# Gating the second half's convolution branch beside the recurrence, dealing rows to 120 blocks, and norming dense tiles one by one

## The chip, the cores and the metric

One NeuronCore (core 0) of one Trainium2 chip. The metric is the device time of one launch in microseconds (us); the time before is the median of three runs.

## The reference, cut to what matters

A decoder block on 1024 tokens of width 1024 (16 meta tokens are put in front and dropped again): two token mixers side by side, a gated sum, and an expert layer.

```python
z = rmsnorm(h, g_mix) @ w_in                       # conv_val, conv_gate, rwkv_in, gate_logits
y_a = conformer_conv(conv_val, conv_gate, ...)     # ... silu(layernorm(conv(u))) @ w_conv_out
y_b = rwkv7_mix(rwkv_in, ...)                      # a recurrence over tokens, then ... @ w_rwkv_out
gate_a, gate_b = split(sigmoid(gate_logits), 2)
h = h + (gate_a * y_a + gate_b * y_b) @ w_o
h = h + peer_ffn(rmsnorm(h, g_ffn), ...)           # 8 heads x top 16 of 128x128 experts per token
out = rmsnorm(h, g_final)[:, 16:]

# peer_ffn, per token t with its 128 chosen experts e:
coef = gate * gelu(x . expert_u[e])
y = sum over e of coef * expert_v[e]
```

## The kernel before, in words

All arithmetic is fp32. A matrix product runs as three TensorE matmuls on a split of each operand into a high and a low part (`mm3`, L226 to L229). The split (`split`, L222 to L224) is a copy on ScalarE (ACT) for the high part and a subtraction on GpSimd (POOL) for the low one. `whalf` (L231) loads half of a 128-column weight tile through SyncE's DMA queue, splits it, and notes the split in a list `paces` that later paces row gathers.

The engines work through their queues in order. A scheduler writes these queues at build time: it takes instructions by the order of the program text, as priority, and by its own estimate of when they can run. Work marked `LATER` has a lower priority and fills gaps.

The tokens are taken in two halves of 512. The first half runs through convolution, recurrence, mix and routing before the second half's recurrence starts. For the second half the order in the text is: `rwkv_inputs(1)`, the recurrence `rwkv(1)` (chunks of small matmuls, L385 to L785, which ends in the tile `carry`, L744), the gates, then

- `gather_coefs` (L1015 to L1033), marked `LATER`: for token tile 3 each of 128 chosen rows of expert_u is gathered (L1027, one gather of 128 x 1024 fp32 on POOL's queue) and multiplied with x and summed on VectorE (DVE, L1029, "dot"). The first 62 rows use a pool of their own, `ga`; the other 66 use the pool `gp`.
- `mix_and_route(1)` (L849 to L975): both branches are projected. The convolution branch `sil` is loaded from DRAM and split as `s2`, the recurrence branch `ogd` as `o2`. Eight output columns m times two branches k, each 12 matmuls of 128x512, are multiplied on DVE with the gates `sga` from DRAM (L902). The k = 0 products of all eight m come first and are kept in `hbuf1`; the k = 1 products follow and are added (L912), split as `m2`, and multiplied with `w_o` (L913 to L932; the residual sum is L929). The queries and the top 16 follow.
- `gather_rows` for token tile 0 (L980 to L1013), `LATER`: per row one gather of 1 MB (expert_u and expert_v row of each of 128 tokens, L1005), a dot (L1008), gelu and gate on ACT (L1009, L1010), and the weighted sum onto `yr` (L1000, "row add"). There are three row buffers.
- `spread_gates` (L1046): gates and coefs of the other five token tiles become dense 128-expert blocks. `u_stage` for 68 blocks.
- `dense` (L1106 to L1179): 32 groups of 4 expert blocks. Per group the gated activations `c` times expert_v (`py`, `zp`, 128x512) are added onto the residual of five token tiles DT = 4, 5, 6, 7, 3 (L1161). Meanwhile the 256 rows of tiles 1 and 2 run through `gather_rows`: 8 are dealt at block 3 and 2 at every later block, so the last ones at block 127.
- The end: the rows left over, then one norm over the five dense tiles at once (L1169, `rstd` L194 to L206: Ln and Exp on ACT, then two small DVE operations), and per tile the product with `g_final`: on DVE (L1177) for t = 0, 2, 4, on ACT and POOL (L1174, L1175) for t = 1, 3. Tile 2's own norm and output (`final`, L1035 to L1043) come with its last row.

Matmuls read the sums of the two tiles `zps` and `acc`, PSUM buffers that are taken in turn.

```python
        early = range(8 * hf)
        kept = [hb1[0][:, m // 2, 512 * (m % 2):512 * (m % 2) + 512] for m in early]
        for m in early:
            mixed(m, 0, s2, kept[m])
        for m in range(8):
            ga = kept[m] if m in early else mixed(m, 0, s2, None)
            gb = mixed(m, 1, o2, None)
            V.tensor_add(gb, gb, ga)
            split(m2[:, 0, m], m2[:, 1, m], gb)
```

## Time and profile before

| what | value |
|---|---|
| time, median of three runs | 3659.9 us (3624.96 to 3678.22) |
| the profiled execution's own time | 3653.25 us |
| its span, first to last instruction | 3651.5 us |
| mean granted TensorE clock | 0.944 |
| busy: TensorE (PE), DVE, POOL, ACT | 90%, 74%, 62%, 43% |
| TensorE instructions | 16175 |

In rows of the profile a line number is one of the kernel before. PE is TensorE, DVE VectorE, ACT ScalarE, POOL GpSimd, SP SyncE. Names stand as result<-operands. In brackets is how long the engine sat idle before the instruction and what ended that. PEclk is the granted TensorE clock, 1.00 for 2.4 GHz and 0.50 for 1.2 GHz. PE's instructions overlap each other, so their starts, not their durations, give the rate.

### The profile page before, as it was taken

How to read it: one execution, taken by the hardware profiler on the slowest of the kernel's cores; microseconds unless marked ns; L12 is line 12 of the kernel's file. 1: busy time of each engine (PE TensorE's matmuls, PEld its weight loads, DVE VectorE, ACT ScalarE, POOL GpSimd, SP SyncE). 2: the span in 40 equal slices, each digit the busy share in tenths (PEclk: the TensorE clock that was granted, in tenths of full speed). 3: DMA queues.
4: the chain of work that ended last, by engine and by line, in shares of the span. 5: the costliest groups of instructions: out<-in, count | busy, mean ns of one | idle time of the engine just before them, and what ended most of it. 6: DMA issues, size and time to landing. Idle time of an engine off the chain costs nothing.

```text
span 3651.5 us, 49244 instructions
## 1 busy us (share of the span) xinstructions
PE 3282.5 (90%) x16175; PEld 2635.6 (72%) x16175; DVE 2684.8 (74%) x5108; ACT 1563.9 (43%) x3714; POOL 2280.4 (62%) x2123
## 2 busy tenths in 40 slices
PE   7999998888788998788899996899999998989994
PEld 7887776677566776676688885777777776777773
DVE  2566538969986775899999887666767666667777
ACT  5555443243444444433367774333333343333333
POOL 3442304535787655656888886676777766767774
PEclk9999979999998899999899998999999999999997
DMA  4321213333677676854699999888889888888987
GB/s 152 113 66 48 60 44 121 107 131 97 199 222 243 180 230 226 308 183 153 215 333 345 351 344 317 285 316 311 319 331 333 332 304 309 319 305 316 329 329 277
DMA packets 347381, 867.66 MB, mean 238 GB/s; under 512 B 53208, under 2 KB 132704, under 8 KB 293876
## 3 DMA queue, kind: packets, MB, share of 16 engines
q0 software_dynamic: 75328, 475.06, 36.0%
q1 hardware_dynamic: 182436, 328.77, 26.9%
q10 hardware_dynamic: 89360, 60.68, 5.4%
q8 instruction: 128, 2.10, 0.2%
q14 instruction: 129, 1.06, 0.1%
HBM read 777.48 MB, written 86.92 MB: 237 GB/s over the span
## 4 chain that ended last, share of the span: by engine, by line
PE 30%; DVE 20%; DMA 13%; issue 10%; POOL 8%; ACT 2%; POOLq 0%; ACTq 0%; DVEq 0%; SPq 0%
DMA row<-euv,idx 6%; PE zp L227 5%; PE zp L229 5%; PE zp L228 5%; PE py L227 3%; PE pg L1088 3%; PE py L228 3%; PE py L229 3%; POOL vlo L224 2%; DVE row L1008 2%; DMA gd<-gt 2%; DVE yr L1000 2%; DVE cy L348 2%; DMA vraw<-euv 2%; POOL row L1027 2%
## 5 line engine op out<-in xcount | busy, mean ns | idle before, releaser
L1005 POOL DMA_INDIRECT row<-euv,idx x384 | 411.2, 1071 | 319.6 <-DVE yr L1000 231.9
L1000 DVE SCALAR_TENSOR_TENSOR yr<-row,act,yr 128x1024 f32<-128x1024 f32 x384 | 493.2, 1284 | 153.9 <-ACT act L1010 151.6
L1008 DVE SCALAR_TENSOR_TENSOR row<-row,xr 128x1024 f32<-128x1024 f32 x256 | 311.5, 1217 | 164.4 <-DMA row<-euv,idx 157.5
L224 POOL TENSOR_TENSOR vlo<-vraw,vhi 128x512 fp32r<-128x512 f32 x256 | 330.8, 1303 | 156.7 <-ACT vhi L223 139.9
L224 POOL TENSOR_TENSOR ul<-ur,uh 128x512 fp32r<-128x512 f32 x256 | 340.3, 1336 | 38.6 <-ACT uh L223 32.2
L1009 ACT ACTIVATE act<-act 128x1 f32<-128x1 f32 x384 | 76.7, 200 | 644.2 <-DVE row L1008 635.3
L227 PE MATMUL py<-vhi,c 128*128 128x512 f32 x640 | 259.0, 409 | 75.8 <-DVE hbuf L1161 32.6
L227 PE MATMUL zp<-x,uh 128*128 128x512 f32 x784 | 315.5, 402 | 7.9 <-ACT g L1101 7.9
L229 PE MATMUL zp<-x,ul 128*128 128x512 f32 x784 | 314.4, 401 | 6.3 <-POOL ul L224 6.3
L228 PE MATMUL zp<-x,uh 128*128 128x512 f32 x784 | 314.4, 401 | 0.0
L229 PE MATMUL py<-vhi,c 128*128 128x512 f32 x640 | 255.6, 406 | 17.0 <-POOL c L224 16.7
L227 PE MATMUL zp<-vhi,c 128*128 128x512 f32 x640 | 251.4, 401 | 21.4 <-DVE hbuf L1161 15.2
L223 ACT ACTIVATE vhi<-vraw 128x512 fp32r<-128x512 f32 x256 | 159.9, 626 | 255.7 <-DMA vraw<-euv 129.4
L228 PE MATMUL py<-vlo,c 128*128 128x512 f32 x640 | 257.1, 402 | 0.4 <-POOL vlo L224 0.4
L228 PE MATMUL zp<-vlo,c 128*128 128x512 f32 x640 | 251.8, 398 | 0.0
L229 PE MATMUL zp<-vhi,c 128*128 128x512 f32 x640 | 249.3, 398 | 0.0
L348 DVE SCALAR_TENSOR_TENSOR cy<-u,vec,cy 128x512 f32<-128x512 f32 x240 | 243.4, 1014 | 5.4
L1008 DVE SCALAR_TENSOR_TENSOR row<-row,xng 128x1024 f32<-128x1024 f32 x128 | 217.4, 1700 | 14.3 <-DMA row<-euv,idx 14.3
L1029 DVE SCALAR_TENSOR_TENSOR row<-row,xng 128x1024 f32<-128x1024 f32 x128 | 184.5, 1447 | 57.4 <-DMA row<-euv,twice 57.1
L1027 POOL DMA_INDIRECT row<-euv,twice x128 | 152.7, 1193 | 111.7 <-DVE row L1029 73.0
L227 PEld LDWEIGHTS py<-vhi,c 128*128 128x128 f32 x640 | 124.3, 194 | 118.6 <-DVE hbuf L1161 43.3
L223 ACT ACTIVATE uh<-ur 128x512 fp32r<-128x512 f32 x256 | 159.3, 625 | 98.6 <-PE zp L228 51.0
(1666 smaller groups left out, 9267.7 us busy)
## 6 DMA issues: line engine op xcount, KB each, us to landing
vraw<-euv SPq DMA_DIRECT2D x256, 256.0 KB, 6.0
ur<-eut SPq DMA_DIRECT2D x256, 256.0 KB, 6.0
gd<-gt ACTq DMA_DIRECT2D x20, 1920.0 KB, 20.8
gblk<-gd SPq DMA_DIRECT2D x30, 1280.0 KB, 11.4
gs<-g SPq DMA_DIRECT2D x68, 256.0 KB, 7.1
g<-gs SPq DMA_DIRECT2D x68, 256.0 KB, 5.9
wbr<-w_in SPq DMA_DIRECT2D x64, 256.0 KB, 3.0
wqr<-w_q SPq DMA_DIRECT2D x64, 256.0 KB, 3.4
```

The source lines that it names most:

```text
L223: A.activation(hi, src, AF.Copy)
L224: return eng.tensor_sub(lo, src, hi.bitcast(F32))
L227: PE.matmul(ps, whi, xhi, start=first, stop=False)
L228: PE.matmul(ps, whi, xlo, start=False, stop=False)
L229: PE.matmul(ps, wlo, xhi, start=False, stop=last)
L348: V.scalar_tensor_tensor(y, u[:, j:j + 512], cw, y, op0=OP.mult, op1=OP.add)
L1000: V.scalar_tensor_tensor(y, row[:, 1], act[:, j:j + 1], y, op0=OP.mult, op1=OP.add)
L1005: G.indirect_dma_start(out=row.rearrange("p a d -> p (a d)"), out_offset=None, in_=a["euv"], in_offset=bass.IndirectOffsetOnAxis(ap=idx[0] ...
L1008: V.scalar_tensor_tensor(row[:, 0], row[:, 0], 1.0, xn, op0=OP.mult, op1=OP.mult, accum_out=aj)
L1027: G.indirect_dma_start(out=row, out_offset=None, in_=a["euv"].rearrange("e (k d) -> (e k) d", k=2), in_offset=bass.IndirectOffsetOnAxis(ap ...
L1029: V.scalar_tensor_tensor(row, row, 1.0, xn, op0=OP.mult, op1=OP.mult, accum_out=act[:, j:j + 1])
L1088: PE.matmul(pg[:, x], o2[:, x], o1[:, x], start=True, stop=True)
```

## The change

Three parts. First, a new function `mix_first` projects the second half's convolution branch right after the gates in the text, so in the midst of the recurrence, multiplies it with its gates and stores eight tiles `mk` (256 KB each) in DRAM; `mix_and_route(1)` loads these and no longer computes them. The pool `gp`, in which the last 66 rows of `gather_coefs` live, is now made after `mix_first` has given its memory back. Second, the 256 rows of tiles 1 and 2 are dealt to the blocks by `NROWS * (b + 1) // LAST`, so that the deal ends at block 119, and what is left over stands before the last group's second half in the text. Third, each dense tile is normed by itself (`last`) as soon as its last sum is there; all five go through DVE.

```diff
+NROWS, LAST = (NGT - 1) * P, 120
...
+    def mix_first(es):
+        sp = pool(es, "es1", side="right")
+        s2 = sp.tile([P, 2, 4, 512], F32R, name="s2e")
+        for c in range(4):
+            o = sp.tile([P, 512], F32, name="lde", bufs=4)
+            SY.dma_start(o, sil[c][1])
+            split(s2[:, 0, c], s2[:, 1, c], o)
+        for m in range(8):
+            _, hi, lo = whalf(a["w_cr"][m], "wc", 0)
+            ps = zps.tile([P, 512], F32, name="zp")
+            for c in range(4):
+                mm3(ps, hi[:, c], lo[:, c], s2[:, 0, c], s2[:, 1, c], c == 0, c == 3)
+            g = sp.tile([P, 512], F32, name="ge", tag="lde", bufs=4)
+            SY.dma_start(g, sga[m][1])
+            V.tensor_mul(g, ps, g)
+            SY.dma_start(mk[m], g)
...
-                    o = sp.tile([P, 512], F32, name="ld", bufs=3)
+                    o = sp.tile([P, 512], F32, name="ld", bufs=3 + hf)
...
-        early = range(8 * hf)
-        wc = [whalf(a["w_cr"][m], "wc", 0) for m in early[:4]]
-        s2 = loaded(mp, sil, "s2", "s2")
+        wc = [whalf(a["w_cr"][m], "wc", 1) for m in range(4 * hf)]
+        if hf:
+            load_x(hb1[0], 4)
+        else:
+            s2 = loaded(mp, sil, "s2", "s2")
...
+                V.tensor_mul(ps, ps, g)
+                V.tensor_add(g, ps, ga)
...
-        for m in early:
-            mixed(m, 0, s2, kept[m])
         for m in range(8):
-            ga = kept[m] if m in early else mixed(m, 0, s2, None)
-            gb = mixed(m, 1, o2, None)
-            V.tensor_add(gb, gb, ga)
+            if hf:
+                ga = sp.tile([P, 512], F32, name="gm", tag="ld", bufs=nld)
+                SY.dma_start(ga, mk[m])
+            else:
+                ga = mixed(m, 0, s2, None)
+            gb = mixed(m, 1, o2, ga)
             split(m2[:, 0, m], m2[:, 1, m], gb)
-        if hf:
-            load_x(hb1[0], 4)
...
+        def last(t, tt):
+            V.tensor_add(ss[:, 0, t:t + 1], ss[:, 0, t:t + 1], ss[:, 1, t:t + 1])
+            r = rstd(cb, ss[:, 0, t:t + 1], 1, 1.0 / D, 1e-6, f"rd{t % 2}")
+            q = cb.tile([P, D], F32, name="yo", tag="c2", bufs=NB + 1)
+            V.scalar_tensor_tensor(q, hb[tt], r, gf, op0=OP.mult, op1=OP.mult)
+            (A if t % 2 else SY).dma_start(out[tt * P:(tt + 1) * P], q)
...
-                for _ in range(0 if b < NB - 1 else 2 * NB if b == NB - 1 else 2):
+                for _ in range(0 if b < NB - 1 else NROWS * (b + 1) // LAST - (NROWS * b // LAST if b >= NB else 0)):
                     next(rows, None)
...
+                if n and g0 == P - NB:
+                    for _ in rows:
+                        pass
+                    tables()
+                    gf = gp.tile([P, D], F32, name="gf", tag="xng", bufs=2)
+                    SY.dma_start(gf, a["g_fin"].to_broadcast([P, D]))
...
-        for _ in rows:
-            pass
...
+                        if n:
+                            last(t, tt)
...
         wp[0] = pool(top, "wp1", 2, side="right")
+        with ExitStack() as e0:
+            mix_first(e0)
+        gp = pool(top, "gp", 1, side="right")
```

On DVE, this is where the second half's recurrence ends, in the kernel before. `am` and `zt` belong to its last chunk, `q2` to `carry` is its closing normalization, `hbuf1` is the gating of the convolution branch, and `yr` a row add of tile 0.

```order
L607 TENSOR_TENSOR am_10906<-bp_10907,rcs_8829 128x256
L607 TENSOR_TENSOR am_10906<-bp_10911,rcs_8829 128x256
L213 SCALAR_TENSOR_TENSOR q2_11010<-pp_11012,q2_11010 128x512
L214 SCALAR_TENSOR_TENSOR oT_10806<-q2_11010,oT_10806 128x512
L739 SCALAR_TENSOR_TENSOR o_11008<-o_11008,ngg_8835,oT_10806 128x512
L744 TENSOR_TENSOR carry_69<-o_11008,pp_11021 128x512
L958 MEMSET F_12755 128x136
L902 TENSOR_TENSOR hbuf1_11914<-zp_12004,ga_12017 128x512
L1000 SCALAR_TENSOR_TENSOR yr_14405<-row_14408,act_14402,yr_14405 128x1024
```

The same place in the changed kernel (L1051 is the dot of `gather_coefs`, L1030 that of `gather_rows`, L1022 the row add, L926 and L927 the product with the gate and the sum with `mk`):

```order
L609 TENSOR_TENSOR am_10914<-bp_10919,rcs_8837 128x256
L1051 SCALAR_TENSOR_TENSOR row_14406,coef_5962<-row_14406,xng_14228 128x1024
...
L1051 SCALAR_TENSOR_TENSOR row_14427,coef_5962<-row_14427,xng_14228 128x1024
L215 SCALAR_TENSOR_TENSOR q2_11018<-pp_11020,q2_11018 128x512
L1054 TENSOR_TENSOR coef_5962<-coef_5962,gate0_5961 128x128
L216 SCALAR_TENSOR_TENSOR oT_10814<-q2_11018,oT_10814 128x512
L741 SCALAR_TENSOR_TENSOR o_11016<-o_11016,ngg_8843,oT_10814 128x512
L746 TENSOR_TENSOR carry_69<-o_11016,pp_11029 128x512
L1030 SCALAR_TENSOR_TENSOR row_14440,act_14434<-row_14440,xng_14432 128x1024
L1022 SCALAR_TENSOR_TENSOR yr_14437<-row_14440,act_14434,yr_14437 128x1024
L926 TENSOR_TENSOR zp_12203<-zp_12203,ga_12216 128x512
L927 TENSOR_TENSOR ga_12216<-zp_12203,gm_12201 128x512
```

Nine dots of `gather_coefs` now stand between the last `am` and `q2` (the first and the last are shown), where none stood, and the first dot of tile 0 stands behind `carry`, where three stood ahead of it.

On PE, the first matmuls of the convolution branch (`s2`) came behind the recurrence's closing matmuls (`pp`) before:

```order
L717 MATMUL bp_10996<-kr_9434,st3_1_10808 128x64
L730 MATMUL pp_11006<-oT_10806,imb_8833 128x512
L736 MATMUL pp_11012<-q2_11010,cst_67 128x512
L227 MATMUL zp_12004<-s2_11971,wch_11949 128x512
L227 MATMUL acc_12020<-s2_11971,wch_11955 128x512
```

In the changed kernel they (`s2e`) stand between matmuls of the recurrence's chunks:

```order
L711 MATMUL bp_9672<-st0_0_9574,nw_9386 64x128
L716 MATMUL bp_9677<-am_9372,tm_9255 64x128
L229 MATMUL zp_11930<-s2e_11907,wch_11926 128x512
L229 MATMUL zp_11953<-s2e_11907,wch_11949 128x512
L635 MATMUL cp__9662<-y_9650,zt_9287 128x128 x4
L595 MATMUL cp__9694<-tm_9571,as_9612 128x64 x2
```

All 96 of them moved some 540 rows up PE's queue, in among chunk work that ran at 1188 to 1230 us in the trace of before.

The end of DVE's queue in the changed kernel (`hr3` is the last dense sum, `rd0` and `rd1` the norms of the dense tiles in turn, `rf` that of tile 2, `sqf` and `yo` outputs):

```order
L206 SCALAR_TENSOR_TENSOR rd0q_31278<-rd0q_31278,rd0m_31276 128x1
L1197 TENSOR_TENSOR hr3_20436<-hr3_20436,py_31375 128x512
L207 SCALAR_TENSOR_TENSOR rd0r_31279<-rd0q_31278,rd0r_31279 128x1
L200 TENSOR_SCALAR rd1m_31305<-ssd_20403 128x1
L1022 SCALAR_TENSOR_TENSOR yr_25615<-row_30535,act_25612,yr_25615 128x1024
...
L1022 SCALAR_TENSOR_TENSOR yr_25615<-row_30661,act_25612,yr_25615 128x1024
L200 TENSOR_SCALAR rfm_30869<-ssf_30866 128x1
L206 SCALAR_TENSOR_TENSOR rfq_30871<-rfq_30871,rfm_30869 128x1
L207 SCALAR_TENSOR_TENSOR rfr_30872<-rfq_30871,rfr_30872 128x1
L1064 SCALAR_TENSOR_TENSOR sqf_30867<-yr_25615,rfr_30872,gq_30878 128x1024
L1146 SCALAR_TENSOR_TENSOR yo_31285<-hbuf1_12127,rd0r_31279,gf_31257 128x1024
L206 SCALAR_TENSOR_TENSOR rd1q_31307<-rd1q_31307,rd1m_31305 128x1
```

Seven row adds now stand behind the last dense sum (ten before), and behind them `rf`, then the four remaining norms one after the other; before, the one norm of five tiles stood among the row adds and only `rf` came last.

## Rows read from the trace of the kernel before

**Rows 1.** Windows: us, busy us (x count) by engine, PEclk, DMA share, GB/s

```profile
1200.00:1250.00 50.00, 45.11 (x253) 36.01 (x253) 34.81 (x60) 22.88 (x61) 35.25 (x51) 0.74 0.60 175
...
2350.00:3550.00 1200.00, 1119.74 (x4738) 898.45 (x4736) 823.06 (x1094) 427.87 (x1092) 848.80 (x796) 0.97 0.88 320
```

**Rows 2.** PE's waits, 1150 to 1500 us: engine, tile, line <- releaser: us, times

```profile
PE zp L227 <- DVE ga L902: 5.1, 3, 3.5
PE pp L516 <- DVE a_s L481: 4.3, 1, 4.3
```

**Rows 3.** Windows around PE's stretches at the lower clock, columns as in rows 1

```profile
1166.40:1188.00 21.60, 21.57 (x84) 17.33 (x85) 8.62 (x16) 3.88 (x11) 8.39 (x11) 0.50 0.71 257
...
1198.80:1212.30 13.50, 13.50 (x52) 10.46 (x49) 7.97 (x14) 11.77 (x32) 10.09 (x18) 0.50 0.63 212
...
1239.40:1253.00 13.60, 13.59 (x54) 11.35 (x55) 10.05 (x18) 4.40 (x12) 5.31 (x8) 0.50 0.76 209
```

**Rows 4.** PE in time order, convolution branch, lower clock: start, us, instruction

```profile
1420.26 0.63 PE L228 MATMUL zp<-s,wch 128*128 128x512 f32 x1
1420.68 0.63 PE L229 MATMUL zp<-s,wcl 128*128 128x512 f32 x1
```

**Rows 5.** PE in time order, convolution branch, full clock

```profile
1430.98 0.39 PE L229 MATMUL zp<-s,wcl 128*128 128x512 f32 x1
1431.20 0.39 PE L227 MATMUL zp<-s,wch 128*128 128x512 f32 x1
```

**Rows 6.** Dots of gather_coefs by line, 1180 to 1300 us (duration ns min/median/max)

```profile
L1029 DVE SCALAR_TENSOR_TENSOR row<-row,xng x39: 1209/1224/2099, 1180.3 to 1297.0; 128x1024 f32<-128x1024 f32 x39
```

**Rows 7.** The same, 1300 to 1370 us, and what they waited for

```profile
L1029 DVE SCALAR_TENSOR_TENSOR row<-row,xng x28: 1215/1226/2234, 1300.9 to 1363.8; 128x1024 f32<-128x1024 f32 x28
...
  DMA row<-euv,twice: 14.3, 15
```

**Rows 8.** DVE in time order, end of the recurrence and the mix

```profile
1407.47 0.69 DVE L213 SCALAR_TENSOR_TENSOR q<-pp,q 128x512 f32<-128x512 f32 x1 [22.15 <-ACT q L212]
...
1412.98 0.69 DVE L744 TENSOR_TENSOR carry<-o,pp 128x512 f32<-128x512 f32 x1 [1.40 <-POOL o L740]
...
1429.50 2.30 DVE L1008 SCALAR_TENSOR_TENSOR row<-row,xng 128x1024 f32<-128x1024 f32 x1
...
1474.20 0.69 DVE L912 TENSOR_TENSOR ga<-ga,hbuf 128x512 f32<-128x512 f32 x1
...
1490.01 0.68 DVE L929 TENSOR_TENSOR hbuf<-hbuf,zp 128x512 f32<-128x512 f32 x1
```

**Rows 9.** Waits, 2350 to 3550 us, columns as in rows 2

```profile
DVE row L1008 <- DMA row<-euv,idx: 150.1, 92, 8.2
POOL row L1005 <- DVE yr L1000: 142.4, 66, 7.2
```

**Rows 10.** DVE in time order, the end

```profile
3602.70 0.68 DVE L1161 TENSOR_TENSOR hr<-hr,py 128x512 f32<-128x512 f32 x1
...
3626.33 1.22 DVE L1008 SCALAR_TENSOR_TENSOR row<-row,xr 128x1024 f32<-128x1024 f32 x1 [5.72 <-DMA row<-euv,idx]
...
3637.20 1.29 DVE L1000 SCALAR_TENSOR_TENSOR yr<-row,act,yr 128x1024 f32<-128x1024 f32 x1 [0.60 <-ACT act L1010]
...
3640.22 1.29 DVE L1000 SCALAR_TENSOR_TENSOR yr<-row,act,yr 128x1024 f32<-128x1024 f32 x1 [0.60 <-ACT act L1010]
...
3646.34 1.28 DVE L1042 SCALAR_TENSOR_TENSOR sqf<-yr,rfr,gq 128x1024 f32<-128x1024 f32 x1
```

**Rows 11.** ACT in time order, the end

```profile
3642.67 1.28 ACT L201 ACT_TABLE_LOAD   x1
3643.97 0.20 ACT L201 ACTIVATE rfr<-rfm 128x1 f32<-128x1 f32 x1
3644.19 1.28 ACT L202 ACT_TABLE_LOAD   x1
```

**Rows 12.** POOL in time order, the end

```profile
3612.30 5.72 POOL L1175 TENSOR_TENSOR yo<-hbuf,gf 128x1024 f32<-128x1024 f32 x2 [3.50 <-ACT hbuf L1174]
```

More of the change, by code (lines that the diff above doesn't have):

```diff
@@ L193, in body @@
     sil = [[dr.tile([P, 512], F32, name=f"sil{j}_{h}") for h in range(2)] for j in range(4)]
+    mk = [dr.tile([P, 512], F32, name=f"mk{m}") for m in range(8)]
     ogd = [[dr.tile([P, 512], F32, name=f"ogd{j}_{h}") for h in range(2)] for j in range(4)]
@@ L855, in mix_and_route @@
             sq = pool(es, "sq1", side=side)
-            mp = pool(es, "mp1", side=side)
+            mp = None
             sp = pool(es, "sp1", side=side)
@@ L884, in loaded, with mixed @@
             return t
-        early = range(8 * hf)
-        wc = [whalf(a["w_cr"][m], "wc", 0) for m in early[:4]]
-        s2 = loaded(mp, sil, "s2", "s2")
+        nld = 3 + hf
+        wc = [whalf(a["w_cr"][m], "wc", 1) for m in range(4 * hf)]
[3 more added lines that the diff above has]
+            s2 = loaded(mp, sil, "s2", "s2")
         o2 = loaded(mo, ogd, "o2", "o2")
         m2 = xt.tile([P, 2, 8, 512], F32R, name="m2", tag="xt")
-        def mixed(m, k, src, o):
-            _, hi, lo = wc[m] if k == 0 and m < len(wc) else whalf(a["w_cr"][m], "wc", k)
+        def mixed(m, k, src, ga):
+            _, hi, lo = wc[m] if k and m < len(wc) else whalf(a["w_cr"][m], "wc", k)
             ps = bank()
@@ L897, in mixed @@
                 mm3(ps, hi[:, c], lo[:, c], src[:, 0, c], src[:, 1, c], c == 0, c == 3)
-            g = sp.tile([P, 512], F32, name="ga", tag="ld", bufs=3)
+            g = sp.tile([P, 512], F32, name="ga", tag="ld", bufs=nld)
             SY.dma_start(g, sga[8 * k + m][hf])
-            if o is None:
-                o = g
-            V.tensor_mul(o, ps, g)
-            return o
-        kept = [hb1[0][:, m // 2, 512 * (m % 2):512 * (m % 2) + 512] for m in early]
-        for m in early:
-            mixed(m, 0, s2, kept[m])
-        for m in range(8):
-            ga = kept[m] if m in early else mixed(m, 0, s2, None)
-            gb = mixed(m, 1, o2, None)
-            V.tensor_add(gb, gb, ga)
+            if ga is None:
+                V.tensor_mul(g, ps, g)
+            else:
+                V.tensor_mul(ps, ps, g)
+                V.tensor_add(g, ps, ga)
+            return g
+        for m in range(8):
+            if hf:
+                ga = sp.tile([P, 512], F32, name="gm", tag="ld", bufs=nld)
+                SY.dma_start(ga, mk[m])
+            else:
+                ga = mixed(m, 0, s2, None)
+            gb = mixed(m, 1, o2, ga)
             split(m2[:, 0, m], m2[:, 1, m], gb)
-        if hf:
-            load_x(hb1[0], 4)
         ss = sp.tile([P, 2, 4], F32, name="ss2")
@@ L929, in mix_and_route @@
                 V.tensor_add(h, h, acc[t])
-                s_ = sp.tile([P, 512], F32, name="sq2", tag="ld", bufs=3)
+                s_ = sp.tile([P, 512], F32, name="sq2", tag="ld", bufs=nld)
                 A.activation(s_, h, AF.Square, accum_out=ss[:, n, t:t + 1])
@@ L939, in mix_and_route @@
         r = rstd(sp, ss[:, 0], 4, 1.0 / D, 1e-6, "r1")
-        dg = sp.tile([P, 4, P], F32, name="dr", tag="ld", bufs=3)
+        dg = sp.tile([P, 4, P], F32, name="dr", tag="ld", bufs=nld)
         for t in range(4):
@@ L963, in mix_and_route @@
                 mm3(ps, hi[:, c], lo[:, c], x2[:, 0, c], x2[:, 1, c], c == 0, c == NCD - 1)
-            q = sp.tile([P, 512], F32, name="qT", tag="ld", bufs=3)
+            q = sp.tile([P, 512], F32, name="qT", tag="ld", bufs=nld)
             A.activation(q, ps, AF.Copy)
@@ L1211, in body @@
         wps.close()
-        gp = pool(top, "gp", 1, side="right")
         nraw[:] = 6, 4
         wp[0] = pool(top, "wp1", 2, side="right")
+        with ExitStack() as e0:
+            mix_first(e0)
+        gp = pool(top, "gp", 1, side="right")
     hr = restore(gp)
```

12 lines of the change are left out of this document (removed).

## The prediction

> **What bounds the kernel now.** I read the busy shares first, then the windows by stage, then what TensorE (PE) waits for, then the stretches in time order. PE is busy 90% of the span, but what bounds differs by stage. In the second half's recurrence PE is busy 45.1 of 50 us at a mean clock of 0.74 [rows 1]: small matmuls, chained to each other through other engines. It stalls once for 4.3 us there [rows 2] and runs three stretches at the 1.2 GHz level, 21.6 + 13.5 + 13.6 = 48.7 us [rows 3]. In `dense` PE is busy 1119.7 of 1200 us [rows 1]: PE sets the pace there, and the rows of tiles 1 and 2 run beside it. At the end nothing but a chain on DVE and ACT is left: the last dense sum starts at 3602.70 and the last instruction ends at 3651.5, 48.8 us later [rows 10]. So the change touches three places: a chain (recurrence), a stage between two chains (mix), and a chain at the end.
>
> **Part one: the convolution branch moves into the recurrence.** The 96 matmuls are the same before and after. At the full clock one follows another after 0.22 us [rows 5], so 96 take some 21.8 us (0.2275 each over a longer run of them); at the lower level the spacing is 0.42 [rows 4], so 41 us. Between chunks of a recurrence that keeps PE busy nine tenths, they are not free: only gaps hide them. The 4.3 us stall [rows 2] lies behind them and can swallow its length; 21.8 − 4.3 = 17.5. The first and second low stretch [rows 3] lie where they go, and I give 2.5 us back, since the stalls ahead of such stretches get fillers. That is +15 us for `carry`. Bounds: +41, if all run at the lower level; −7, if all three low stretches vanish (half of 48.7 is 24.4, and 17.5 − 24.4 = −6.9).
>
> DVE gets eight products of about 0.7 us in between (as `hr` and `ga` cost, [rows 8, 10]); POOL and ACT get the splits that they had later; DRAM gets eight stores and eight loads of 256 KB. The DMA share in that window is 0.60 [rows 1], so 4 MB at the 175 GB/s of that row are hidden there; nobody waits for `mk` until after `carry`. I cost them at nothing; without that cover it is 4 MB over 175 GB/s, 24 us of queue, but spread over 200 us.
>
> The price that I find only in the order: `gp` is now made after `mix_first`, so the last 66 dots of `gather_coefs` start among recurrence work that ran at 1240 to 1263 before, some 1255 with the shift, where the 39 dots of the earlier window start at 1180.3 [rows 6]. They took 62.9 us over 27 intervals, 2.33 each, late in the recurrence [rows 7], and 116.7 over 38, 3.07 each, earlier [rows 6]. 65 intervals end at 1406 or 1455. `q`, the head of the closing chain, ran at 1407.47 after DVE had idled for 22.15 us [rows 8]; with +15 it is due at 1422. Nine of the dots stand right ahead of it, and queued behind it on DVE are `oT`, `o` and `carry`, for which the `o2` split on POOL and all of the mix wait. So the hold is 0 below 1422 and +33 at the other end. The stretch that it falls into is mostly that of the faster rate, so I take +3.
>
> **The mix after `carry`.** Before, from `carry` (1412.98) to the last sum L912 (1474.20) it took 61.2 us, and to the first residual sum (1490.01) 77.0 [rows 8]. PE did 96 matmuls of each branch there. Now it does half: 21.8 us for `o2`. But DVE becomes the limit: ten dots and ten row adds of tile 0 stand among the eight products and eight sums, 10 x (1.3 to 2.3) + 10 x 1.29 + 16 x 0.69 = 37 to 47 us (a dot took 2.30 [rows 8], 1.22 at best [rows 10]; row add 1.29 [rows 10]; product 0.69 [rows 8]). Before, three of the dots lay ahead of `carry`. So the last sum comes 37 to 47 us behind `carry`: a gain of 14 to 24, of which PE gives back nothing, since `w_o` wants the same tiles in the same order; the 5.1 us that PE waited for `ga` [rows 2] are inside it. I take −18, nearer the slow end, because the gathers feed those dots through the same three buffers. Bounds: −24, and 0 if the row stream alone paces it as before. From there to `dense` the same work stands in the same order: 0, with 5 to either side.
>
> **Part two: the deal.** It works only if rows wait to be dealt. In `dense` DVE waits 150.1 us for gathered rows, and POOL's next gather waits 142.4 us for a row add that frees a buffer [rows 9]: the stream runs at the pace of three buffers, not of the deal. The order agrees: row adds come at the same rate per dense sum, some three ahead of before all along, and seven are left behind the last dense sum instead of ten. So 0 for `dense`, 10 to either side for its overlaps.
>
> **Part three: the end.** I count from the last dense sum's old start, S. It now stands behind `rd0`, whose two table loads of 1.28 us [rows 11] start only when the first dense tile is summed: S + 1.8 (0 to 5). Then seven row adds at the steady distance of 3.02 us (3637.20 to 3640.22, [rows 10]): the first starts 1.3 us later, six distances and 1.29 follow, so S + 22.5, and S + 24 with some wait for a gather (22 to 27). Before, the last one ended at S + 38.8, with a 5.72 us wait [rows 10] behind POOL's two products of 5.72 us [rows 12], which go. From there to the end of `sqf` it is 6.1 us as before (3641.51 to 3647.62, [rows 10]). Then the gain is spent: four norms, one after the other. A norm's chain on ACT is 3.25 us (3642.67 to 3645.92, [rows 11]), two small DVE steps 0.4, the product 1.28 [rows 10]. The first overlaps `sqf`: 3.2 beyond it. Then 4.9, 3.6 and 4.9, since an output on ACT's queue that waits for its product holds the next norm's loads in two cases, and the third starts beside a product. Sum 16.6, and 3.9 for the last output (3647.62 to 3651.5). S + 24 + 6.1 + 16.6 + 3.9 = S + 50.6, against S + 48.8: +2, range −6 to +10.
>
> A rule speaks against this part. The Trainium skill, "ScalarE: Activation LUTs", section "What ACT_TABLE_LOAD costs", says that a switch costs a load of about 1.28 us and a drain of about 1.38 more. The first half agrees with the row; the second does not: Ln starts at 3643.97, 0.02 us after the load's end [rows 11]. By the page the eight loads of the four norms would cost some 11 us more (an estimate from that page) and the forecast would be 3666; I go by the row. The same page, section "Table sets: the hidden batching unit", has one set that holds both ln and exp; here both functions load one each, in the trace and in the changed order, so 1.28 us of each chain of 3.25 is a load that this rule would save.
>
> **Sum.** Against the profiled execution's own 3653.25 us: +15 +3 −18 +0 +2 = +2, so 3655 us. That run is 0.2% under the median of 3659.9, so the forecast is "no change"; about 2%, 73 us, is what a measurement of this kernel can tell from none.
>
> **Rivals.**
> 1. The coefs hold the closing chain (slower). One mechanism: 66 dots on DVE ahead of `q`. Beyond 1422 − 1255 = 167 us over 65, 2.57 us per row, each 0.1 us costs 6.5. At the 3.07 of [rows 6], +33 in place of +3: 3685. For it: the dots share DVE and the gather queue with a recurrence that also got `mix_first`'s loads. Against it: 2.33 in [rows 7], and the 22 us in which DVE idled. Chance 0.2.
> 2. PE's clock (faster). [rows 3] show PE all but fully busy at 0.50 there, and the last of the three stretches begins as the 4.3 us stall [rows 2] ends. If 96 wide matmuls keep it at 1.00 there, up to 24.4 us come back instead of 2.5: 3655 − 22 = 3633. The Trainium skill, "TensorE: Matmul & The Clock Gate", section "What's actually happening", says that activity releases the throttle, which would make it so. Against it: PE was no less busy in the low stretches of [rows 3] than anywhere, and they lasted 13 to 22 us all the same. Chance 0.15.
> 3. The row stream keeps up with the deal (faster): if row adds end with block 119 or soon after, the seven at the end go, 18 to 21 us, and `sqf` overlaps the dense norms, 6 and more. 3655 − 28 = 3627. For it: PE and not DVE bounds `dense`. Against it: [rows 9]. Chance 0.1.
> 4. The change does not do what it says. For the deal that is part of my forecast.
>
> My forecast has 0.55: 3632 to 3680 by its own terms. The range, 3612 to 3692, takes in rivals 1 to 3 and the bounds. Over 2% either way needs two rivals at once or something that I don't see: faster 0.08, slower 0.08, within 2% 0.84.
>
> **What would show it.** Right: `carry` 10 to 25 us later than before; the first residual sum about where it was; PE's window at 1200 fuller; seven row adds after the last dense sum, then five norms in a line with two loads each, ending about 50 us after it. Wrong: `q` starting on the heels of a dot; the three low stretches gone; DVE's wait for rows in `dense` much under 150 us; a `dense` stage of another length, for which I have no term.

## The result and the profile after

The changed kernel takes 3678.8 us (median of 20 runs, 3663.7 to 3697.1), the kernel before 3654.5 (20 runs, 3619.6 to 3682.9). The ratio is 1.0079, 95% interval 1.0059 to 1.0099: slower by 0.8%, where the forecast was no change with a sum of +2 us. The time lies inside the stated range of 3612 to 3692, but the interval of the ratio leaves "no change" out. The profiled execution has a span of 3675.2 us, 23.7 more than before.

Five stages tell where it went. They are cut at DVE instructions that every kernel of this study has: the last scan of the decays in the second half (`cs`, 1142.85 before), `carry`, the last residual sum, the first and the last dense sum, the end. Times in us:

| stage | before | after | difference |
|---|---|---|---|
| scan to `carry` (recurrence) | 270.1 | 294.3 | +24.2 |
| `carry` to last residual sum (mix) | 102.2 | 92.6 | −9.6 |
| to first dense sum (routing, spreading) | 757.0 | 771.3 | +14.3 |
| dense | 1330.5 | 1327.6 | −2.9 |
| last dense sum to the end | 48.8 | 52.3 | +3.5 |

The execution after reached the scan 5.7 us earlier, in work that the change does not touch. DVE in time order, the cuts up to dense, first before, then after (columns as in [rows 8], which hold `carry` at 1412.98 and the first residual sum at 1490.01 before):

```profile
1142.85 1.34 DVE L454 TENSOR_TENSOR_SCAN cs<-rcs,w_s 128x512 f32<-128x512 f32 x1
...
1515.18 0.68 DVE L929 TENSOR_TENSOR hbuf<-hbuf,zp 128x512 f32<-128x512 f32 x1
...
2272.18 0.68 DVE L1161 TENSOR_TENSOR hbuf<-hbuf,py 128x512 f32<-128x512 f32 x1
```

```profile
1137.18 1.22 DVE L456 TENSOR_TENSOR_SCAN cs<-rcs,w_s 128x512 f32<-128x512 f32 x1
...
1415.80 1.23 DVE L1051 SCALAR_TENSOR_TENSOR row<-row,xng 128x1024 f32<-128x1024 f32 x1
...
1426.83 0.69 DVE L215 SCALAR_TENSOR_TENSOR q<-pp,q 128x512 f32<-128x512 f32 x1 [9.80 <-ACT q L214]
...
1431.51 0.69 DVE L746 TENSOR_TENSOR carry<-o,pp 128x512 f32<-128x512 f32 x1 [1.38 <-POOL o L742]
...
1482.21 0.68 DVE L927 TENSOR_TENSOR ga<-zp,gm 128x512 f32<-128x512 f32 x1
...
1495.80 0.69 DVE L951 TENSOR_TENSOR hbuf<-hbuf,zp 128x512 f32<-128x512 f32 x1 [1.10 <-PE zp L231]
...
1524.10 0.67 DVE L951 TENSOR_TENSOR hbuf<-hbuf,zp 128x512 f32<-128x512 f32 x1
...
2295.35 0.68 DVE L1197 TENSOR_TENSOR hbuf<-hbuf,py 128x512 f32<-128x512 f32 x1
```

The last dot of `gather_coefs` (L1051) ended 9.8 us before `q` could start, and `q` waited for ACT: the dots did not hold the closing chain.

PE's stretches at the lower clock answer to [rows 3]. Windows of after:

```profile
1160.00:1175.00 15.00, 12.66 (x49) 10.32 (x50) 8.45 (x12) 2.39 (x7) 12.96 (x16) 0.50 0.80 259
1175.00:1360.00 185.00, 179.86 (x1208) 138.70 (x1207) 115.21 (x203) 76.65 (x202) 93.46 (x135) 1.00 0.61 189
1360.00:1385.00 25.00, 25.00 (x88) 16.83 (x89) 13.51 (x22) 5.52 (x14) 9.85 (x9) 0.50 0.58 181
...
1404.00:1420.00 16.00, 14.99 (x52) 10.31 (x53) 7.55 (x13) 5.10 (x14) 5.67 (x6) 0.50 0.69 232
```

With the 96 wide matmuls among the chunks the clock stayed at 2.4 GHz from 1175 to 1360, but two low stretches came later, 15 + 25 + 16 = 56 us in all. PE had stalled for 7.5 us just before 1162, and for 1.3 and 2.3 us before 1348 and 1360. Before, there was a fourth low stretch of 6.8 us that [rows 3] do not hold, so 48.7 becomes 55.5:

```profile
1297.90:1304.70 6.80, 6.80 (x25) 5.41 (x24) 4.08 (x9) 2.41 (x5) 5.01 (x7) 0.50 0.80 242
```

Over the whole stage from the scan to `carry` the granted clock is about the same, 0.89 before and 0.90 after, and PE's busy time grew with the stage. Before, after, and a run that leaves the 96 matmuls out (no_mm, below):

```profile
1142.80:1413.00 270.20, 253.41 (x1583) 196.43 (x1582) 167.47 (x294) 109.87 (x278) 147.06 (x187) 0.89 0.63 194
```

```profile
1137.20:1431.50 294.30, 277.98 (x1669) 210.45 (x1667) 172.82 (x296) 109.01 (x278) 149.76 (x197) 0.90 0.65 208
```

```profile
1141.00:1421.20 280.20, 261.41 (x1580) 198.35 (x1578) 172.96 (x299) 112.50 (x285) 161.11 (x197) 0.85 0.69 220
```

In dense the same waits stand as in [rows 9], a little shorter; a row add still frees the buffer for which POOL waits:

```profile
POOL row L1027 <- DVE yr L1022: 140.7, 65, 7.1
DVE row L1030 <- DMA row<-euv,idx: 125.9, 73, 8.4
```

The end, DVE in time order (compare [rows 10]): the last dense sum, the last row add, the output of tile 2, then the five dense outputs.

```profile
3622.91 0.68 DVE L1197 TENSOR_TENSOR hr<-hr,py 128x512 f32<-128x512 f32 x1
...
3644.39 1.29 DVE L1022 SCALAR_TENSOR_TENSOR yr<-row,act,yr 128x1024 f32<-128x1024 f32 x1 [0.60 <-ACT act L1032]
...
3650.52 1.28 DVE L1064 SCALAR_TENSOR_TENSOR sqf<-yr,rfr,gq 128x1024 f32<-128x1024 f32 x1
3651.72 1.28 DVE L1146 SCALAR_TENSOR_TENSOR yo<-hbuf,rd0r,gf 128x1024 f32<-128x1024 f32 x1
...
3655.40 1.28 DVE L1146 SCALAR_TENSOR_TENSOR yo<-hbuf,rd1r,gf 128x1024 f32<-128x1024 f32 x1
...
3660.85 1.28 DVE L1146 SCALAR_TENSOR_TENSOR yo<-hbuf,rd0r,gf 128x1024 f32<-128x1024 f32 x1
...
3664.62 1.28 DVE L1146 SCALAR_TENSOR_TENSOR yo<-hbuf,rd1r,gf 128x1024 f32<-128x1024 f32 x1
...
3670.07 1.28 DVE L1146 SCALAR_TENSOR_TENSOR yo<-hr,rd0r,gf 128x1024 f32<-128x1024 f32 x1
```

The last row add starts 21.5 us behind the last sum and ends 22.8 behind it, near the 24 of the forecast, and then four norms follow at distances of 3.7 and 5.5 us. ACT shows the longer ones: the next load waits behind the output that waits for its product.

```profile
3656.72 0.36 ACTq L1147 DMA_DIRECT2D out<-yo  x1
3657.11 1.28 ACT L203 ACT_TABLE_LOAD   x1 [2.13 <-DVE yo L1146]
```

### The profile page after: what moved, and what is told of

It is laid out like the page before. It is cut to its first block, busy times and chain, and to the rows that moved or that the text cites. A ratio compares the mean times of both kernels' runs of the same rounds, so it can differ in the third digit from the quotient of the medians.

```text
span 3675.2 us, 49349 instructions
## 1 busy us (share of the span) xinstructions
PE 3307.2 (90%) x16175; PEld 2640.6 (72%) x16175; DVE 2667.8 (73%) x5126; ACT 1568.9 (43%) x3731; POOL 2258.5 (61%) x2121
## 4 chain that ended last, share of the span: by engine, by line
PE 46%; DVE 22%; DMA 14%; issue 9%; POOL 8%; ACT 2%; POOLq 0%; ACTq 0%; DVEq 0%; SPq 0%
PE zp L229 7%; PE zp L231 7%; PE zp L230 7%; DMA row<-euv,idx 4%; DVE cy L350 4%; PE py L229 3%; PE py L230 3%; PE py L231 3%; PE pg L1110 3%; DMA gd<-gt 2%; DMA g<-gs 2%; DVE yr L1022 2%; DVE row L1030 2%; DMA vraw<-euv 2%; POOL vlo L226 2%
## 5 line engine op out<-in xcount | busy, mean ns | idle before, releaser
L1022 DVE SCALAR_TENSOR_TENSOR yr<-row,act,yr 128x1024 f32<-128x1024 f32 x384 | 492.9, 1284 | 147.7 <-ACT act L1032 141.4
L1027 POOL DMA_INDIRECT row<-euv,idx x384 | 400.1, 1042 | 313.3 <-DVE yr L1022 224.8
L1030 DVE SCALAR_TENSOR_TENSOR row<-row,xr 128x1024 f32<-128x1024 f32 x256 | 311.1, 1216 | 138.7 <-DMA row<-euv,idx 134.4
L231 PE MATMUL zp<-x,ul 128*128 128x512 f32 x784 | 318.5, 406 | 16.4 <-POOL ul L226 16.4
L231 PE MATMUL py<-vhi,c 128*128 128x512 f32 x640 | 257.3, 409 | 23.8 <-POOL c L226 23.7
L1051 DVE SCALAR_TENSOR_TENSOR row<-row,xng 128x1024 f32<-128x1024 f32 x128 | 190.2, 1490 | 57.5 <-DMA row<-euv,twice 57.1
L1030 DVE SCALAR_TENSOR_TENSOR row<-row,xng 128x1024 f32<-128x1024 f32 x128 | 202.3, 1580 | 23.7 <-DMA row<-euv,idx 23.7
```

What stands on the lines that cost most here:

```text
L231: PE.matmul(ps, wlo, xhi, start=False, stop=last)
L1022: V.scalar_tensor_tensor(y, row[:, 1], act[:, j:j + 1], y, op0=OP.mult, op1=OP.add)
L1027: G.indirect_dma_start(out=row.rearrange("p a d -> p (a d)"), out_offset=None, in_=a["euv"], in_offset=bass.IndirectOffsetOnAxis(ap=idx[0] ...
L1030: V.scalar_tensor_tensor(row[:, 0], row[:, 0], 1.0, xn, op0=OP.mult, op1=OP.mult, accum_out=aj)
L1051: V.scalar_tensor_tensor(row, row, 1.0, xn, op0=OP.mult, op1=OP.mult, accum_out=act[:, j:j + 1])
```

## Experiments

All ratios are to the kernel before on the same chip. The stages are those of the table above, from one profiled execution each; "rows" are row adds ahead of the first and behind the last dense sum.

| run | ratio (95%) | recurrence | mix | to dense | dense | end | rows |
|---|---|---|---|---|---|---|---|
| before | 1 | 270.1 | 102.2 | 757.0 | 1330.5 | 48.8 | 120, 10 |
| after | 1.0079 (1.0059 to 1.0099) | 294.3 | 92.6 | 771.3 | 1327.6 | 52.3 | 124, 7 |
| a_only | 1.0033 (1.0001 to 1.0065) | 286.7 | 95.2 | 770.1 | 1320.3 | 40.6 | 124, 7 |
| b_only | 0.9982 (0.9946 to 1.0018) | 273.3 | 108.3 | 764.6 | 1333.4 | 48.4 | 120, 10 |
| c_only | 1.0042 (1.0014 to 1.0071) | 275.6 | 106.4 | 758.3 | 1322.8 | 55.2 | 120, 11 |
| bc_only | 1.0060 (1.0034 to 1.0086) | 279.2 | 105.5 | 760.1 | 1335.3 | 62.1 | 120, 10 |
| no_mm | 1.0062 (1.0034 to 1.0091) | 280.2 | 98.9 | 788.5 | 1322.7 | 45.4 | 128, 5 |
| after_align | 1.0054 (1.0025 to 1.0083) | 309.6 | 92.7 | 770.2 | 1332.4 | 52.1 | 124, 7 |
| before_mis | 0.9991 (0.9967 to 1.0015) | 272.1 | 104.6 | 757.4 | 1320.3 | 48.4 | 120, 10 |
| before_allal | 0.9995 (0.9967 to 1.0023) | 282.2 | 106.4 | 753.8 | 1318.5 | 48.4 | 120, 10 |
| a_allal | 1.0016 (0.9987 to 1.0045) | 297.3 | 95.1 | 769.4 | 1320.1 | 41.0 | 124, 7 |
| p_29 | 1.0059 (1.0034 to 1.0085) | 316.7 | 93.3 | 754.8 | 1338.6 | 57.4 | 116, 13 |
| d_tail | 1.0004 (0.9970 to 1.0038) | 268.5 | 106.0 | 756.2 | 1336.3 | 49.6 | 120, 10 |
| n4 | 1.0100 (1.0072 to 1.0127) | 307.7 | 109.0 | 784.2 | 1328.5 | 22.7 | 134, 0 |
| n4bc | 1.0068 (1.0047 to 1.0089) | 304.2 | 113.7 | 791.0 | 1333.7 | 14.4 | 134, 0 |
| x4vB | 1.0166 (1.0124 to 1.0208) | 298.6 | 106.1 | 756.1 | 1417.9 | 21.6 | 120, 0 |
| x4v | 1.0136 (1.0094 to 1.0179) | 284.6 | 106.4 | 760.0 | 1413.1 | 16.6 | 120, 0 |
| x4w | 0.9959 (0.9930 to 0.9989) | 297.1 | 91.8 | 757.0 | 1349.7 | 14.4 | 119, 0 |

The recurrence of one order of instructions varies by tens of us between executions (268.5 to 298.6 over the nine executions that have neither `mix_first` nor fewer weight buffers), so a single pair does not settle that column. The columns "to dense" and "end" repeat within some 10 and 1 us and follow the rows.

**One part at a time.** a_only undoes the second and third part of the change:

```diff
-                for _ in range(0 if b < NB - 1 else NROWS * (b + 1) // LAST - (NROWS * b // LAST if b >= NB else 0)):
+                for _ in range(0 if b < NB - 1 else 2 * NB if b == NB - 1 else 2):
...
-                        if n:
-                            last(t, tt)
+        r = rstd(cb, ss[:, 0], NDT, 1.0 / D, 1e-6, "rd")
```

> The first part alone: convolution branch beside the recurrence, the deal and the end as before. Theory 1 (the recurrence is bound by PE and pays for the 96 matmuls, the mix gives back about 10 us): carry 18 to 25 us later than before, first residual sum 8 to 12 us later, 10 to 16 us slower in all. Theory 2 (the loss comes from the end, the recurrence's is given back whole): within 5 us of before.

b_only puts the new deal and the drain ahead of the last group's second half into the kernel before:

> The deal alone, with the left-over rows ahead of the last group's second half. Theory 1 (the row stream runs at the pace of its three buffers): no difference, within 5 us, and the same number of row adds behind the last dense sum within two. Theory 2 (the dealing held rows back): 15 us faster or more.

c_only puts `last` there and takes the common norm out; bc_only takes both:

> The end alone: each dense tile normed by itself on DVE. Theory 1 (the four serial norms cost more than POOL's stall gave): 4 to 8 us slower, from the last dense sum to the end 53 to 57 us. Theory 2 (the loss of the changed kernel is all in the first part): within 3 us, 48 to 50 us from the last dense sum to the end.

> The second and third part of the change together with three row buffers. Theory (ten row adds are still left behind the last dense sum, and the norms come behind them one after the other): the end 53 to 57 us in place of 48, 5 to 9 us slower than before, as with the third part alone. Rival (the deal and the drain take rows off the end): the end 46 to 50 us, same time as before.

The first part costs 0.3%, 12 us of 3655, the third 0.4%, 15 us, the deal nothing that can be measured: it changes neither the rows ahead of dense nor those behind it. Theory 1 gave the time of a_only, b_only without a difference and the end of c_only (55.2 us; as a whole c_only lost more than the 4 to 8 us expected, with an interval of 5 to 26). It did not give where a_only's `carry` and first residual sum stand: they came 0.2 us later and 10 us earlier than before, since that execution had reached the scan 16 us earlier; only the lengths of the stages (+16.6 and −7.0) have the signs of the theory. It did not give bc_only either, whose end of 62.1 us and loss of 0.6% (22 us) lie beyond both expectations; what makes it longer than c_only's is not shown. One surprise: a_only's end is 8 us shorter than before's, as three rows fewer are left there. So the norms one by one cost the changed kernel 52.3 − 40.6 = 11.7 us of its end, hidden by those rows in the sum.

**Is it PE's time that the recurrence pays?** no_mm leaves the 96 matmuls of `mix_first` out, so `mk` holds the gated input in place of the projection:

```diff
-            ps = zps.tile([P, 512], F32, name="zp")
-            for c in range(4):
-                mm3(ps, hi[:, c], lo[:, c], s2[:, 0, c], s2[:, 1, c], c == 0, c == 3)
+            ps = s2[:, 0, m % 4].bitcast(F32)
```

> The changed kernel whose mix_first leaves out its 96 matmuls (the gates are multiplied with the split input instead of the projection); loads, splits, products and stores stay. Theory 1 (PE's own time): carry 17 to 25 us earlier than in the changed kernel, and the whole 15 to 25 us shorter. Theory 2 (the later start of gp's dots, the splits on POOL and ACT or the added DMA delay the recurrence): carry within 5 us of the changed kernel.

The recurrence fell by 14 us to 280.2, and by more against the mean of the five executions with the matmuls (300.9). Since the granted clock differs from one execution to the next, I also multiplied each recurrence with its mean clock: an estimate of its length at the full clock, as if all of it went with the clock, as the spacing of matmuls does in [rows 4] and [rows 5]. By that the nine without `mix_first` lie at 231 to 243 us, no_mm at 239, and the five with the matmuls at 257 to 265. So the growth, some 25 us, is the 96 matmuls' time on PE, as theory 1 says; the later dots, the splits and the added DMA, which no_mm keeps, leave it inside the spread of the nine. The size that theory 1 gave for the whole did not come: `carry` stood 10 us earlier than in the changed kernel, not 17 to 25, and the whole did not fall, since the stage to dense took 788.5 us. It had 128 row adds in it. That pointed to the rows.

**The rows taken ahead of dense.** p_29 is a_only with one number changed, so that tile 0's paced rows come later:

```diff
-    pace = {PACE0 + k: paces[2 * k + 5] for k in range(14)}
+    pace = {PACE0 + k: paces[2 * k + 29] for k in range(14)}
```

> The first part of the change alone, with the paced gathers of tile 0 tied to later weight halves, so that by the order 116 row adds stand ahead of the first dense sum in place of 124 (120 before the change) and 13 behind the last one in place of 7. Theory 4 (between the routing and dense the DMA queues are full, so each row taken there costs 3 us, and each one left behind the last dense sum costs 3 too): from the last residual sum to the first dense sum 745 to 750 us in place of 770, the end 18 us longer (59), the whole as without the pacing within 6 us. Theory 5 (that stage is longer for another reason, the later start of the gates' spreading or the tiles' places): 765 to 772 us.

Eight rows fewer made the stage 15.3 us shorter and the end 16.8 longer. The end came about as theory 4 has it (57.4 us for 59); the stage, 754.8 us, lies between the 745 to 750 of theory 4 and the 765 to 772 of theory 5, and the whole is 0.6% slower than before, where a_only is 0.3%, with intervals that overlap. To see which rows did it I divide the stage in two behind the last index of the top 16 on DVE (`ti`): first the routing, then the spreading of the gates and `u_stage`. Windows of the two parts (columns as in [rows 1]), before, after, p_29:

```profile
1515.20:1734.70 219.50, 184.87 (x855) 152.47 (x855) 214.04 (x879) 82.40 (x169) 120.37 (x85) 0.94 0.55 188
1734.70:2272.20 537.50, 485.68 (x2696) 414.69 (x2696) 480.24 (x846) 332.71 (x882) 443.71 (x378) 0.96 0.92 317
```

```profile
1524.10:1746.80 222.70, 193.05 (x864) 157.10 (x865) 214.50 (x877) 82.20 (x169) 118.17 (x85) 0.92 0.55 190
1746.80:2295.30 548.50, 489.96 (x2689) 414.91 (x2687) 490.07 (x858) 334.63 (x890) 447.22 (x382) 0.96 0.91 318
```

```profile
1552.90:1759.20 206.30, 180.63 (x833) 147.70 (x834) 189.07 (x848) 76.96 (x148) 104.89 (x73) 0.93 0.47 158
1759.20:2307.70 548.50, 494.42 (x2720) 420.97 (x2718) 494.73 (x863) 337.89 (x895) 452.67 (x385) 0.96 0.92 320
```

The two parts have different limits. In the routing DVE is busy 214 of 219.5 us and the DMA share is 0.55: DVE sets the pace. It holds 21 row adds before and after; the eight that p_29 moved stood there, and it fell by 16.4 us, 2 us per row. In the second part the DMA share is 0.92 and the rate 317 GB/s. There the changed kernel has 84 row adds in place of 80 and takes 11 us longer, and p_29 has 84 too and takes the same 548.5 us. So p_29 did not undo the growth: it made up for it in the other part, and the reason that theory 5 gives is not excluded by it. The spreading of the gates does start later, 240.8 us behind the last residual sum before, 314.0 after and 298.2 in p_29. Its first product on DVE, before and after:

```profile
1755.98 0.67 DVE L1076 TENSOR_TENSOR o2h<-gT,keys 128x512 f32<-128x512 f32 x1
```

```profile
1838.12 0.68 DVE L1098 TENSOR_TENSOR o2h<-gT,keys 128x512 f32<-128x512 f32 x1
```

That rows by themselves lengthen the second part is seen in two runs that come below, x4w and n4. They have the same number of weight buffers, and in both the spreading starts early (230 and 235 us behind the last residual sum), but 82 and 88 row adds stand in the part:

```profile
1744.30:2287.90 543.60, 492.12 (x2713) 422.46 (x2712) 485.38 (x852) 334.56 (x887) 447.16 (x381) 0.95 0.92 322
```

```profile
1782.60:2346.00 563.40, 497.63 (x2688) 420.11 (x2687) 491.24 (x874) 342.51 (x906) 453.01 (x387) 0.95 0.94 321
```

That is 19.8 us for six rows, 3.3 each, while the rate hardly changes; the four rows of the changed kernel would be 13 us by this, and 11 were measured. So theory 4 can account for the whole growth, with a DMA that moves 317 to 322 GB/s in this part whatever its length. That the later spreading has no share in it is not shown.

**A theory that fell: the place of the weight tiles.** The change moves the pool of the weights by allocating `gp` later. Products with them came slower: PE in time order, the first and last of 96 products in a row of `u_stage`, in the kernel before (21.55 us over 95 distances, 226.8 ns each) and in before_mis (22.16, 233.3 ns; after has 233.3 too):

```profile
2554.54 0.39 PE L227 MATMUL zp<-x,uh 128*128 128x512 f32 x1
...
2576.09 0.39 PE L229 MATMUL zp<-x,ul 128*128 128x512 f32 x1
```

```profile
2548.31 0.39 PE L227 MATMUL zp<-x,uh 128*128 128x512 f32 x1
...
2570.47 0.40 PE L229 MATMUL zp<-x,ul 128*128 128x512 f32 x1
```

Four kernels pad pools by 32 bytes in two places and keep the order of instructions; where the tiles then start is my count from the pools' sizes:

```diff
+        pool(top, "pad0", 1, side="right").tile([P, 8], F32, name="pad0")
         wp[0] = pool(top, "wp1", 2, side="right")
```

> The changed kernel with 32 bytes of padding per partition ahead of the pool wp1 and 32 behind gp: the second half's weight tiles start at a multiple of 64 bytes again, as before the change; every engine's order of instructions is that of the changed kernel. Theory 3 (the place of the weight tiles, moved by gp's later allocation, slows each of some 3650 wide matmuls by 5 to 6 ns): spacing of the products with uh, ul and wqh back from 233.5 to 228 ns, 15 to 22 us shorter than the changed kernel. Theory 1 (the order in the route and spread stage, with 14 more row adds ahead of dense): within 4 us of the changed kernel.

> The kernel before with the same 64 bytes of padding, so placed that wp1's weight tiles start 32 bytes off a multiple of 64; the order of instructions is that of before. Theory 3: spacing of the products with uh, ul and wqh up from 228 to 233, 15 to 22 us slower than before. Theory 1: within 4 us of before.

> The kernel before with padding that puts the first half's weight tiles and normalized inputs (wp0, hn0, hn1), which stand 32 bytes off, at multiples of 64 too; same order. Theory 3, if it holds for the first half: its wide matmuls (some 3000 at 230 to 231 ns) come to 227, 5 to 12 us faster than before. Theory 1: within 4 us of before.

> The first part of the change alone (deal and end as before) with all weight tiles at multiples of 64 bytes. Theory 3: 20 to 30 us faster than the same without padding, so 5 to 15 us faster than before. Theory 1: within 4 us of the same without padding, so 10 to 16 slower than before.

The spacing follows the tiles' place as theory 3 says (after_align 228.9 ns), the time does not: before_mis has slower products and 0.9991 of the time, where theory 3 wanted 15 to 22 us more, and its stage to dense is 757.4 us. The padded after_align and a_allal lie 9 and 6 us below the same kernels without padding, with intervals that overlap. Windows from the midst of the stage, before and before_mis:

```profile
1900.00:2150.00 250.00, 249.53 (x1484) 219.25 (x1483) 225.68 (x409) 183.81 (x489) 214.76 (x195) 1.00 1.00 346
```

```profile
1900.00:2150.00 250.00, 250.00 (x1482) 218.69 (x1481) 225.10 (x409) 183.41 (x487) 213.28 (x194) 1.00 1.00 344
```

PE shows as busy throughout in both, at a DMA share of 1.00: the slower products filled slack that this busy time does not show. (The 14 more row adds of the expectation are four by the trace, 124 and 120.)

**The end.** d_tail gives all five outputs of the kernel before to DVE (L1174 and L1175 go):

> The kernel before with one edit: the outputs of all five dense tiles on DVE, none on ACT and POOL. Theory (POOL's 5.7 us of products hold up the last gathers): the end 42 to 45 us in place of 48, 3 to 6 us faster. Rival (the two more products on DVE cost what POOL's stall did): same.

The rival was right: 49.6 us. POOL's stall is not what the end costs. That the ten rows are, the next runs show. n4 and n4bc take four row buffers in place of three:

```diff
-NROW = 3
+NROW = 4
...
-        nraw[:] = 6, 4
+        nraw[:] = 4, 3
```

> The kernel before with four row buffers in place of three, paid for with fewer weight buffers (4 raw and 3 split halves in place of 6 and 4); the deal is as before. Theory 4 (the row stream is bound by its buffers, not by the deal): no row add left behind the last dense sum, the end 15 to 22 us in place of 48, and 15 to 30 us faster unless the missing weight buffers stall PE. Rival (DMA binds the row stream in dense too): dense grows by what the end gains, same time.

> The second and third part of the change (deal over 120 blocks, dense tiles normed one by one) with four row buffers. Theory 4: as with four buffers alone within 5 us, since the deal changes no instruction's place there; the five norms one by one start before the last sum and end 15 to 20 us after it. Rival (the deal matters once the buffers don't bind): 5 us or more faster than four buffers alone.

No row is left behind the last sum, dense keeps its length, and the end falls to 22.7 and 14.4 us. The last row add of n4 comes 166.8 us ahead of the last dense sum (3674.55):

```profile
3507.78 1.28 DVE L1000 SCALAR_TENSOR_TENSOR yr<-row,act,yr 128x1024 f32<-128x1024 f32 x1
```

It is 166.8 us in n4bc too, where the deal ends eight blocks earlier: in dense buffers bind the stream, not the deal. n4bc is some 12 us faster than n4 (with intervals that overlap), 8 of them at the end, where the norms one by one follow on the last sum. Both are slower than before all the same: 14 rows more lie ahead of dense and the recurrence stalls in two places on ACT, once for 8.7 us:

```profile
PE cp__9964 L620 <- ACT at L671: 8.7, 1, 8.7
PE cp__10379 L620 <- ACT at L671: 4.4, 1, 4.4
```

So the fourth buffer was given to dense alone, first at the cost of two split buffers of expert_v (x4v with the second and third part of the change, x4vB without):

```diff
+                row = xp.tile([P, 2, D], F32, name="rowx") if xp and j % 4 == 3 else gp.tile([P, 2, D], F32, name="row", bufs=nrow)
...
-NV2 = 6
+NV2 = 4
```

> The second and third part of the change without the first, and a fourth row buffer in dense alone, paid for there with four split buffers of expert_v in place of six; up to dense the order is that of before. Theory 4 (three buffers bind the row stream in dense, and the rows left over are what the end costs): no row add behind the last dense sum, the end 14 to 18 us in place of 48, dense 1320 to 1335 us as before, 25 to 35 us faster. Rival (PE needs the six split buffers, or DMA binds the stream): dense 10 to 30 us longer, within 10 us of before.

> The kernel before with the fourth row buffer in dense alone (four split buffers of expert_v), the deal and the end as before. Theory 4: the end 20 to 24 us in place of 48, 20 to 27 us faster than before, and 6 to 10 us slower than with the norms one by one, since the single norm waits for the last sum. Rival (the norms one by one cost more in any case): as fast as or faster than with them.

The rival of x4v was right in kind, but its size was 10 to 30 us: dense grew by 83 us, and PE waits for just those splits. Both runs are over 1% slower than before; the end is 16.6 us with the norms one by one and 21.6 without.

```profile
PE py L228 <- ACT vhi L224: 46.8, 10, 5.9
PE py L229 <- POOL vlo L225: 27.3, 28, 2.7
```

With weight buffers paying instead (`nraw[:] = 4, 3`, NV2 back at 6):

> The second and third part of the change without the first, and a fourth row buffer in dense alone, paid for with weight buffers (4 raw and 3 split halves in place of 6 and 4) and not with those of expert_v. Theory 4 (buffers bind the row stream in dense): no row add behind the last dense sum, the end 14 to 18 us in place of 48, dense 1320 to 1335 us; from routing to dense up to 10 us more for the missing weight buffers; 15 to 35 us faster than before. Rival (PE's loss in dense came from the added row traffic, not from the split buffers): dense 20 us longer or more, not faster than before.

x4w is faster than before by 0.4% (15 us) and than the changed kernel by some 1.2%. No row add is left behind the last dense sum and the end is 14.4 us. Dense is 1349.7 us, 19 more than before and past the forecast; PE waits there most for ACT's half of the split of `c`:

```profile
PE py L228 <- ACT c L224: 49.9, 20, 6.2
```

So buffers bind the stream in dense. What lengthens dense by 19 us and takes part of the gain back is not shown: n4 has the same wait for `c` (53.8 us over dense) with a dense of 1328.5.

## Why the prediction was wrong

- **The recurrence, +15 and +3 for the dots:** the mechanism was right, the size too small. The five executions with the matmuls lie at 286.7 to 316.7 us (mean 300.9), the nine others of the same order there at 268.5 to 298.6 (mean 278.3): about +23, or +25 at like clock by the estimate above. The step that failed here is "the 4.3 us stall [rows 2] lies behind them and can swallow its length", with the 2.5 us for the clock: 96 x 0.2275 is 21.8, and no part of it came back. The stall on `a_s` went (after has no wait on it), but other stalls took its place: PE's waits from the scan to `carry` are 16.5 us in all before and 14.9 after. The 4.3 us were also not the only stall before: the 7.5 us of after answer to 5.2 us just ahead of the first low stretch.
- **`carry` 10 to 25 us later, a sign of being right:** it came 18.5 us later, which is +15 and +3 almost to the microsecond, by luck. The stage grew by 24.2, and this execution had reached it 5.7 us earlier.
- **The dots:** they did not hold `q` (9.8 us to spare), so the rival of the coefs is out, and the +3 with it.
- **The mix, −18:** right in kind: DVE's row adds and dots stand ahead of the sums, and PE waits for `ga` there, 12.0 and 7.0 us:

```profile
PE acc L229 <- DVE ga L927: 12.0, 2, 7.0
...
PE zp L229 <- DVE ga L927: 7.0, 2, 5.0
```

  It gave 61.2 − 50.7 = 10.5 us up to the last sum and 9.6 to the last residual sum, inside the 0 to 24 stated and short of the 14 to 24 that the sum of DVE's work gave; over the same nine and five executions the means are 105.8 and 93.8. The sum left out DVE's own waits: it is busy for 37.2 of these 50.7 us, as the low end of that sum has it, and idle for the rest, once for 3.96 us for a gathered row.

```profile
1431.50:1482.20 50.70, 29.88 (x91) 21.67 (x92) 37.16 (x46) 15.52 (x38) 33.20 (x25) 0.77 0.87 314
```

  x4w has a mix of 91.8 us without `mix_first`, so the column can fall in another way too.
- **"From there to dense the same work stands in the same order: 0, with 5 to either side":** this is the step that failed most, +14.3 us in this execution and +12 by the means (770.2 over after, a_only, after_align and a_allal, 758.2 over the nine). Neither the work nor its order is the same: four more row adds of tile 0 stand ahead of the first dense sum, and the spreading of the gates starts 73 us later. I counted rows behind the last dense sum only, where three fewer look like a gain. Of the growth 11 us lie behind the routing. Rows cost 3.3 us each there between x4w and n4, so four could cost all of it; what the later spreading adds is open. p_29 does not tell, as it gained its time in the routing.
- **The deal, 0:** right (0.9982, interval across 1). But the order was no sign of it: the three rows fewer at the end come with the first part (a_only has seven there, b_only ten).
- **The end, +2:** right (+3.5), and term by term: the last row add 21.5 us behind the last sum (24 forecast to its end, 22.8 measured), from the end of `sqf` to the end of the last product 19.6 us where 16.6 was the forecast. But the two halves of the sum were larger than its total: three rows fewer gave 8 us, the norms took 11.7. That POOL's products go gave nothing by itself (d_tail).
- **The clock:** part of that rival came, a full clock from 1175 to 1360, and was given back in two later stretches. It brought nothing: 0.89 before, 0.90 after over the recurrence.
- **What can be told from none:** the forecast took 2%, 73 us, for that. With 20 runs of each kernel the interval was 0.2% to either side, so 0.8% shows.
- **ACT's tables:** no drain shows behind a load here either (Ln starts at 3658.40, 0.01 us after the end of the load at 3657.11), so the row was the right guide. Of the other rule of the Trainium skill ("ScalarE: Activation LUTs", section "Table sets: the hidden batching unit": one set holds ln and exp) x4w shows what it is worth. ACT in time order there, one load and then a norm without any:

```profile
3623.83 1.28 ACT L180 ACT_TABLE_LOAD   x1
...
3633.54 0.18 ACT L202 ACTIVATE rd0r<-rd0m 128x1 f32<-128x1 f32 x1
3633.76 0.20 ACT L203 ACTIVATE rd0r<-rd0r 128x1 f32<-128x1 f32 x1
```

  Its last three outputs start 2.5 to 2.9 us apart, in place of 3.7 and 5.5. In after, the gelus of leftover rows come behind `tables()`, and each norm loads twice.

## What to carry to other kernels

When work is moved off a chain, count what the freed place lets in: here the stage behind the mix took in four more gathers of 1 MB and a later start of the spreading, and grew by as much as the mix had gained (+12 and −12 us by the means). Divide such a stage where its limits change before you say what paces it: its mean of 280 GB/s shows neither DVE's part nor the other. Cost matmuls that are put among a chain at their full length unless a stall of PE is shown to take them. Norm tiles one by one only once nothing else is left behind them; with rows still to come, one norm of all tiles hides better (an end of 14.4 and 16.6 us against 22.7 and 21.6 with no row left, 55.2 against 48.8 with rows left).
